# A hybrid decoder layer on one core: small matmuls on column tiles, the forget gate on ScalarE, corrections as biases, and the residuals' mean on GpSimd

## The chip, the cores and the metric

The kernel runs on one core of one Trainium2 chip. The metric is the device time of one execution in microseconds (us); the median of several runs is compared. TensorE (PE in the profile) multiplies matrices, VectorE (DVE), ScalarE (ACT) and GpSimd (POOL) compute elementwise, SyncE (SP) starts transfers.

## The reference

One layer of a decoder (width 2048) is computed for 16 meta tokens, a prompt of 256 tokens and 8 sample tokens, each of which has a past state of its own:

```
x <- LN1(alpha*x + 0.5*SwiGLU_1(x))
x <- LN2(alpha*x + Mixer(x))
x <- LN3(alpha*x + 0.5*SwiGLU_2(x))
Mixer: z = x @ w_in, ten parts of width 2048
  retention (8 heads of 256): rotary q, k; scores q k^T times a decay per head; layer norm per head
  HGRN2 (16 heads of 128): f = lb + (1-lb)*sigmoid(f_h), k = 1 - f, q = silu(q_h), decay prod(f); rms norm per head
  y = sigmoid(a_r)*o_r*silu(g_r) + sigmoid(a_h)*o_h*silu(g_h);  y @ w_out
```

The outputs are the layer's result for the prompt and the samples and the two branches' new states. All inputs are float32, and the feed-forward width is 5504.

## The kernel before, in words

**Dense products.** All 280 tokens lie as columns of tiles with 128 features on the partitions (264 columns where the meta tokens are no longer needed). A weight arrives in units of eight 128x128 blocks (tile `raw`, 512 KB, a transfer of SP's queue, three buffers). ScalarE rounds it to `whi` (L187, type fp32r), VectorE subtracts to get the rest, `wlo` (L188). Activations are split in the same way (`xh`/`xl`, `hh`/`hl`, `yh`/`yl`). Each block then takes three matmuls in `dense` (L217): whi on the high part, whi on the low part, wlo on the high part. A split activation is kept as `Halves`: its left and right half of the columns are read alternately, one column of each in turn, and `pairs` and `apart` lay the output in PSUM out accordingly.

**Order.** The program runs through the first feed-forward layer (`up`, `dn`), norm 1, the mixer, `w_out` (`wo`), norm 2, the second feed-forward layer and norm 3. The order of TensorE's instructions is the order in which the code issues them; the other engines' queues are ordered by a scheduler with priorities. The mixer goes through eight units u, each with one retention head and two HGRN2 heads. A unit's projections are f, q_h, i_h (`pj_f` and so on), then q_r, k_r, v_r, then the gates g_r, a_r, g_h, a_h. `mix_hg` (L717) and `mix_ret` (L952) are generators: after each dense step `pump` counts them down, and a `yield n` asks for n dense steps before the next piece. So the small matmuls stand one group at a time between dense ones, and a group that waits holds all dense work behind it.

**Norm 1 and norm 2.** The first two groups of projections behind a norm multiply x·g before its mean and variance are known. `Norm.first` (L366) and `second` (L383) run them, and `corrected` (L388) puts them right afterwards, with y = -(r·(mean·wg - o)) + wb, where two extra columns of the product give wg and wb. Three VectorE steps do this for each output: a scalar_tensor_tensor, `mul` by r, and at L399 the times -1 plus wb. `first` then goes over the 16 residual tiles d0 to d15: it subtracts the mean at L378 (the helper `sub`, L243) and multiplies by g and r = 1/std at L379. `normalise` (L402) makes the split inputs of everything that follows from these tiles. The mean is the row tile `lnc`, r is `rr`.

**HGRN2.** `evacuate` (L624) turns projections into f, k = 1 - f (both 128x2x280), q and v. f is a sigmoid on ScalarE and a multiply-add on VectorE (L628), k a multiply-add on VectorE (L631). `mix_hg` copies k to K (L723, VectorE), which is later scaled in place. The parts of v are transposed on TensorE for both heads h: two blocks of 128 columns and the 16 columns at each end, four transposes per head into the bank `pt` (L755). The causal scores are built by levels of block size s = 1, 2, 4, 8, 16, 32, 64. The products of neighbours for s = 1 and 2 are split into two tiles and summed over partitions by a matmul with ones (`sums`, L234, banks `pd` and `pl`). For s = 16, 32 and 64 the matmuls K x Q run for each head and block (L803, L798, L793). L803 takes all 128 columns of K at once, so that most of the result is unwanted and a masked VectorE copy (L856, with mask 4) picks the diagonal blocks; L798 puts the two blocks of 32 on two column tiles of the array (`tile_position`), and ScalarE copies the results into `acc` (L851).

**Retention.** After transposes of v and k, `mix_ret` computes the scores `psc` (L996): two wide blocks of 256 and 144 columns and a third with 16 keys and 16 columns. `psr` (L1013) is the new state, seven matmuls of 256 columns per half. Later `pqr` (L1044) multiplies the eight samples' queries, alone in tiles of 32 columns, with their states; samples 0 to 3 and 4 to 7 go to the two halves of a bank, which VectorE adds.

Of the kernel before, what the change touches and what calls it, by code (L numbers as in the profile page):

```python
# [18 lines left out]
P = 128  # L19
# [26 lines left out]
MASKED = 5  # L46

MASKS = {1: [0], 2: [1, MASKED], 4: [2], 8: [3, MASKED + 1], 16: [4]}
# [79 lines left out]
def trunk(ctx: ExitStack, tc: tile.TileContext, A, O):  # L128
# [98 lines left out]
    def sums(out, hilo, part=slice(None)):  # L227

        for i, x in enumerate(hilo):
            if isinstance(x, Halves):  # L230
                o, x = pairs(out), x[:]
            else:
                o, x = out, x[:, part]
            nc.tensor.matmul(o, ones_r, x, start=i == 0, stop=i == 1)  # L234

    def mul(out, a, b):
        nc.vector.tensor_tensor(out=out, in0=a, in1=b, op=ALU.mult)

# [29 lines left out]
    class Norm:  # L268
# [96 lines left out]
        def first(self, block, outs, x0s):  # L365
# [10 lines left out]
            for c in range(KC):  # L376
                d = self.d[c]
                sub(d, d, self.mean)  # L378
# [9 lines left out]
        def corrected(self, outs, x0s, into=()):  # L388
            ys = []
            for i, (o, x0) in enumerate(zip(outs, x0s)):  # L390
# [6 lines left out]
                mul(y, y, self.r[:, x0:])  # L397
                to = into[i] if i < len(into) else y
                nc.vector.tensor_scalar(out=to, in0=y, scalar1=-1.0, scalar2=wgb[:, 1:2], op0=ALU.mult, op1=ALU.add)  # L399
                ys.append(to)  # L400
# [52 lines left out]
    def ffn(i, block, w_dn, which, before=None):  # L453
# [3 lines left out]
        with tc.tile_pool(name=f"h{i}", bufs=1) as hp:  # L457
            hh, hl = [None] * FC, [None] * FC
            for gn, grp in enumerate(ffn_up_groups()):
# [4 lines left out]
                else:  # L464
                    dense(block, KC, outs, xh, xl, cols, parts_in_turn=gn == 0)
                ng = len(grp) // 2
                for j in range(ng):
                    m = grp[j][1]
                    sg = hp.tile([P, n], F32, tag="sg", name=f"sg{m}", bufs=2)
                    nc.scalar.activation(sg, outs[j][:, :n], AF.Silu)  # L470
                    mul(sg, sg, outs[ng + j][:, :n])
# [60 lines left out]
    with tc.tile_pool(name="yp", bufs=1) as yp:  # L532
# [7 lines left out]
        with tc.tile_pool(name="mp", bufs=1) as mp:  # L540
# [37 lines left out]
            vsm = tmp("vsm", (P, 2, P))  # L578
# [26 lines left out]
            def project(groups):  # L605
                for grp in groups:
# [9 lines left out]
                    else:  # L616
                        dense(block, KC, outs, xh, xl, [slice(x0, T) for x0 in x0s], pump)
                    for j in range(0, len(grp), 2):
                        w = T - x0s[j]
                        evacuate(grp[j][0], grp[j][1], grp[j + 1][1], outs[j][:, :w], outs[j + 1][:, :w])  # L620

            def evacuate(n, c0, c1, o0, o1):
                if n == "f":
                    f = tmp("f", (P, 2, T))  # L624
                    k = tmp("k", (P, 2, T))
                    for j, (c, o) in enumerate(((c0, o0), (c1, o1))):
                        nc.scalar.activation(f[:, j, :], o, AF.Sigmoid)
                        nc.vector.tensor_scalar(  # L628
                            out=f[:, j, :], in0=f[:, j, :], scalar1=olb[:, c : c + 1], scalar2=lb[:, c : c + 1],
                            op0=ALU.mult, op1=ALU.add)  # L630
                    nc.vector.tensor_scalar(out=k, in0=f, scalar1=-1.0, scalar2=1.0, op0=ALU.mult, op1=ALU.add)  # L631
# [577 lines left out]
```

## Time and profile before

| what | value |
|---|---|
| median of 3 runs | 2615.33 us (2613.51 to 2615.54) |
| the profiled execution | 2614.54 us, span 2612.5 us, granted TensorE clock 0.999 |
| busy: PE, DVE, ACT, POOL | 2593.6, 1738.4, 1355.4, 3.3 us |
| transfers | 536.26 MB, mean 205 GB/s |
| casts whi and subtractions wlo, all forms | 870 of 1042 ns on ACT, 869 of 1223 ns on DVE |

The profile is one execution. The span goes from its first to its last instruction; some 2 us of the execution lie outside it. A row of a group gives line, engine, operation, output<-inputs and shapes, and then the busy time, the mean of one in ns, and the engine's idle time just before these instructions with what ended it. A row of the waits gives the waiting engine's tile and line, the engine and tile that it waited for, and then the sum in us, the count and the longest. A row of the timeline gives the start, the time up to the last end, and how many instructions of the kind followed one another.

### The profile page before, as it was taken

The page shows a single profiled execution, that of the slowest core. Times are in us where ns is not written, and L with a number is a line of the kernel's source. Part 1 is how long each engine was busy: PE and PEld are TensorE (multiplying, and loading weights), DVE is VectorE, ACT ScalarE, POOL GpSimd, SP SyncE. Part 2 cuts the span into 40 slices and gives each one's busy share as a digit, 9 for nine tenths or more (in the row PEclk, how much of TensorE's full clock was granted, in tenths as well). Part 3 has the DMA queues.
Part 4 walks back from the last instruction along what each step waited for, and adds up shares of the span by engine and source line. Part 5 has one row for each costly group of instructions (what it writes and reads, how often), then busy time and mean ns, then how long its engine had stood idle before and what let it go on. Part 6 is the DMA issues. An engine that isn't in the chain of part 4 may idle for free.

```text
span 2612.5 us, 54486 instructions
## 1 busy us (share of the span) xinstructions
PE 2593.6 (99%) x22576; PEld 2564.1 (98%) x22576; DVE 1738.4 (67%) x2961; ACT 1355.4 (52%) x2120; POOL 3.3 (0%) x38
## 2 busy tenths in 40 slices
PE   9999999999999999999999999999999999999999
PEld 9999999999999999999999999999999999999998
DVE  6554444565579788787878787876995555556555
ACT  5444444444455566656565656565564444444444
POOL 0000000000000000000000000000000000000000
PEclk9999999999999999999999999999999999999999
DMA  7556555556566686767676767666656666666664
GB/s 243 185 185 186 184 184 184 185 186 184 182 195 212 231 271 206 245 212 245 214 249 213 249 215 237 216 232 193 192 181 204 195 197 195 195 194 194 197 198 148
DMA packets 154584, 536.26 MB, mean 205 GB/s; under 512 B 17696, under 2 KB 25696, under 8 KB 154336
## 3 DMA queue, kind: packets, MB, share of 16 engines
q1 hardware_dynamic: 154048, 532.50, 63.4%
q8 instruction: 176, 2.88, 0.4%
q14 instruction: 72, 0.59, 0.1%
q10 hardware_dynamic: 288, 0.29, 0.0%
HBM read 502.12 MB, written 30.61 MB: 204 GB/s over the span
## 4 chain that ended last, share of the span: by engine, by line
PE 89%; DVE 6%; DMA 3%; ACT 2%; issue 1%; SPq 0%; DVEq 0%; ACTq 0%
PE up L217 34%; PE dn L217 18%; PE wo L217 3%; PE pj_q_r L217 3%; PE pj_g_r L217 3%; PE pj_v_r L217 3%; PE pj_f L217 3%; PE pj_k_r L217 3%; PE pj_i_h L217 3%; PE pj_q_h L217 3%; PE pj_a_r L217 3%; PE pj_g_h L217 2%; PE pj_a_h L217 2%; DVE wlo L188 2%; DMA smr<-in_sr 1%
## 5 line engine op out<-in xcount | busy, mean ns | idle before, releaser
L188 DVE TENSOR_TENSOR wlo<-raw,whi 128x1024 fp32r<-128x1024 f32 (+1 forms) x869 | 1061.4, 1223 | 723.5 <-ACT whi L187 721.2
L187 ACT CAST whi<-raw 128x1024 fp32r<-128x1024 f32 (+1 forms) x870 | 904.7, 1042 | 919.4 <-PE up L217 426.7
L217 PE MATMUL up<-xh,wlo 128*128 128x280 f32 (+1 forms) x2624 | 726.0, 280 | 0.8 <-DVE wlo L188 0.6
L217 PE MATMUL up<-xh,whi 128*128 128x280 f32 (+1 forms) x2624 | 725.7, 280 | 0.0
L217 PE MATMUL up<-xl,whi 128*128 128x280 f32 (+1 forms) x2624 | 725.4, 279 | 0.0
L217 PEld LDWEIGHTS up<-xh,wlo 128*128 128x128 f32 x2624 | 492.6, 189 | 1.7 <-DVE wlo L188 1.6
L217 PEld LDWEIGHTS up<-xh,whi 128*128 128x128 f32 x2624 | 492.8, 189 | 0.0
L217 PEld LDWEIGHTS up<-xl,whi 128*128 128x128 f32 x2624 | 492.6, 189 | 0.0
L217 PE MATMUL dn<-hh,whi 128*128 128x280 f32 (+1 forms) x1376 | 384.7, 280 | 0.0
L217 PE MATMUL dn<-hl,whi 128*128 128x280 f32 (+1 forms) x1376 | 384.3, 279 | 0.0
L217 PE MATMUL dn<-hh,wlo 128*128 128x280 f32 (+1 forms) x1376 | 384.3, 279 | 0.0
L217 PEld LDWEIGHTS dn<-hh,whi 128*128 128x128 f32 x1376 | 260.1, 189 | 0.1
L217 PEld LDWEIGHTS dn<-hl,whi 128*128 128x128 f32 x1376 | 260.1, 189 | 0.1
L217 PEld LDWEIGHTS dn<-hh,wlo 128*128 128x128 f32 x1376 | 260.1, 189 | 0.0
L217 PE MATMUL pj_g_r<-xh,whi 128*128 128x264 f32 x256 | 76.7, 300 | 0.0
L217 PE MATMUL pj_v_r<-xh,whi 128*128 128x280 f32 x256 | 74.3, 290 | 0.0
L217 PE MATMUL pj_g_h<-xh,whi 128*128 128x264 f32 x256 | 73.5, 287 | 0.0
L217 PE MATMUL pj_k_r<-xh,wlo 128*128 128x280 f32 x256 | 72.7, 284 | 0.3
L217 PE MATMUL pj_k_r<-xh,whi 128*128 128x280 f32 x256 | 72.7, 284 | 0.0
L217 PE MATMUL pj_v_r<-xl,whi 128*128 128x280 f32 x256 | 72.7, 284 | 0.0
L217 PE MATMUL pj_v_r<-xh,wlo 128*128 128x280 f32 x256 | 72.7, 284 | 0.0
L217 PE MATMUL pj_g_h<-xh,wlo 128*128 128x264 f32 x256 | 71.0, 277 | 1.6 <-DVE wlo L188 1.6
(401 smaller groups left out, 5281.5 us busy)
## 6 DMA issues: line engine op xcount, KB each, us to landing
raw<-in_w_up SPq DMA_DIRECT2D x343, 512.0 KB, 3.9
raw<-in_w_in SPq DMA_DIRECT2D x320, 512.0 KB, 4.1
raw<-in_w_dn SPq DMA_DIRECT2D x172, 512.0 KB, 3.5
smr<-in_sr SPq DMA_DIRECT2D x32, 512.0 KB, 5.3
out_srs<-smr SPq DMA_DIRECT2D x32, 512.0 KB, 5.1
raw<-in_w_out SPq DMA_DIRECT2D x32, 512.0 KB, 3.5
smh<-in_sg SPq DMA_DIRECT2D x16, 512.0 KB, 4.5
vbr<-vrd SPq DMA_DIRECT2D x16, 512.0 KB, 5.6
```

Of the source, the lines that this page charges most:

```text
L187: nc.scalar.copy(hi[:, j:jn, :], raw[:, j:jn, :])
L188: nc.vector.tensor_tensor(out=lo[:, j0:j1, :], in0=raw[:, j0:j1, :], in1=hi[:, j0:j1, :].bitcast(F32), op=ALU.subtract)
L217: nc.tensor.matmul(o, w, t, start=start, stop=stop)
```

## The change

1. **Norms 1 and 2.** `first` subtracts the mean from d0 to d15 with `nc.gpsimd` in place of VectorE; multiplying by g and r stays on VectorE. In `corrected` the `mul` by r becomes a scalar_tensor_tensor that also multiplies by -1. The last step, adding wb, goes away: `corrected` returns (y, wb), and the consumers take wb as the bias of their ScalarE activation or as a scalar of their VectorE multiplication (`mul_biased`). Only v, in `second`, still has it added at once.
2. **Forget gate.** The multiply-add for f, the one for k, and the copy from k to K go to ScalarE.
3. **Transposes of v.** GpSimd collects the ends of v for both heads in a tile `ends` (128 x 64 elements), which one transpose then turns; per unit there are five transposes in place of eight.
4. **Level 16** runs on four column tiles of the array with 32 columns each, in 16 matmuls of 16 columns; ScalarE copies the results as for s = 32. Mask 4 goes, and with it its part of the transfer and the cast at the start. **Level 64** puts its two blocks b on two column tiles.
5. **Third score.** It moves from `psc` to the bank of `pqr`, right ahead of its matmuls, and its product with the decay and its split move along. The two halves of `pqr` now sum up in the bank, and the VectorE addition goes.
6. **Order of columns.** The moving operands of `sums` with two parts (`pd` and s = 2) and of `psr` are read alternately from their two halves, as in `dense`; the readers of the result take the columns apart again.

The diff, cut to its core:

```diff
-MASKED = 5
-MASKS = {1: [0], 2: [1, MASKED], 4: [2], 8: [3, MASKED + 1], 16: [4]}
+MASKED = 4
+MASKS = {1: [0], 2: [1, MASKED], 4: [2], 8: [3, MASKED + 1]}
 ...
     def sums(out, hilo, part=slice(None)):
+            elif len(x.shape) == 3 and x[:, part].shape[1] == 2:
+                o, x = pairs(out), x[:, part].rearrange("p a b -> p b a")
 ...
+    def mul_biased(out, o, b, x):
+        if b is None:
+            mul(out, x, o)
+        else:
+            nc.vector.scalar_tensor_tensor(out=out, in0=o, scalar=b, in1=x, op0=ALU.add, op1=ALU.mult)
 ...
         def first(self, block, outs, x0s):
-                sub(d, d, self.mean)
+                nc.gpsimd.tensor_tensor(out=d, in0=d, in1=self.mean, op=ALU.subtract)
 ...
         def corrected(self, outs, x0s, into=()):
-                mul(y, y, self.r[:, x0:])
-                to = into[i] if i < len(into) else y
-                nc.vector.tensor_scalar(out=to, in0=y, scalar1=-1.0, scalar2=wgb[:, 1:2], op0=ALU.mult, op1=ALU.add)
-                ys.append(to)
+                nc.vector.scalar_tensor_tensor(out=y, in0=y, scalar=-1.0, in1=self.r[:, x0:], op0=ALU.mult, op1=ALU.mult)
+                if i < len(into):
+                    nc.vector.tensor_scalar(out=into[i], in0=y, scalar1=wgb[:, 1:2], scalar2=None, op0=ALU.add)
+                ys.append((y, wgb[:, 1:2]))
 ...
-                        nc.scalar.activation(f[:, j, :], o, AF.Sigmoid)
-                        nc.vector.tensor_scalar(
-                            out=f[:, j, :], in0=f[:, j, :], scalar1=olb[:, c : c + 1], scalar2=lb[:, c : c + 1],
-                            op0=ALU.mult, op1=ALU.add)
-                    nc.vector.tensor_scalar(out=k, in0=f, scalar1=-1.0, scalar2=1.0, op0=ALU.mult, op1=ALU.add)
+                        nc.scalar.activation(f[:, j, :], o, AF.Sigmoid, **bias(b))
+                        nc.scalar.activation(f[:, j, :], f[:, j, :], AF.Identity, scale=olb[:, c : c + 1], bias=lb[:, c : c + 1])
+                    nc.scalar.activation(k, f, AF.Identity, scale=-1.0, bias=1.0)
 ...
             def mix_hg(u, f, k, q, v):
+                ends = tmp("ends", (P, 2, 2, NMETA))
+                nc.gpsimd.tensor_copy(ends[:, :, 0, :], v[:, :, :NMETA])
+                nc.gpsimd.tensor_copy(ends[:, :, 1, :], v[:, :, T - NMETA :])
-                nc.vector.tensor_copy(K, k[:, :, :LP])
+                nc.scalar.copy(K, k[:, :, :LP])
 ...
-                    for b, (t0, n) in enumerate(((NMETA, P), (NMETA + P, P), (0, NMETA), (T - NMETA, NMETA))):
-                        nc.tensor.transpose(pt[:n, b * P : (b + 1) * P], v[:, h, t0 : t0 + n], ident)
+                    for b in range(2):
+                        nc.tensor.transpose(pt[:, b * P : (b + 1) * P], v[:, h, NMETA + b * P : NMETA + (b + 1) * P], ident)
+                    x = pt[:64, 2 * P : 3 * P]
+                    if h:
+                        nc.tensor.transpose(x, ends.rearrange("p c a t -> p (c a t)"), ident)
 ...
                             if s == 64:
+                                j = 64 * b
                                 nc.tensor.matmul(
-                                    pl[0:s, o : o + s], K[:, h, k0 : k0 + s], Q[:, h, q0 + s : q0 + 2 * s],
-                                    start=True, stop=True)
-                            elif s == 32:
-                                for j in (0, 64):
+                                    pl[j : j + s, h * s : (h + 1) * s], K[:, h, k0 : k0 + s], Q[:, h, q0 + s : q0 + 2 * s],
+                                    start=True, stop=True, tile_position=(0, j))
+                            else:
+                                for j in range(0, P, 2 * s):
                                     nc.tensor.matmul(
                                         pl[j : j + s, o : o + s], K[:, h, k0 + j : k0 + j + s],
                                         Q[:, h, q0 + j + s : q0 + j + 2 * s], start=True, stop=True, tile_position=(0, j))
 ...
-                        nc.tensor.matmul(pst[:, :256], kk, vv, start=i == 0, stop=i == 6)
+                        nc.tensor.matmul(pairs(pst[:, :256]), kk, vv.rearrange("p c f -> p f c"), start=i == 0, stop=i == 6)
 ...
                 pq = mx_bank("pqr")
+                scores(pq[:, 256:], 2)
-                                pq[32 * j : 32 * j + 32, 256 * e : 256 * e + 256], qdr[:, c, 32 * b : 32 * b + 32],
-                                sms[2 * e + c][:, j, :], start=c == 0, stop=c == 1, tile_position=(0, 32 * j))
+                                pq[32 * j : 32 * j + 32, :256], qdr[:, c, 32 * b : 32 * b + 32],
+                                sms[2 * e + c][:, j, :], start=e + c == 0, stop=e + c == 2, tile_position=(0, 32 * j))
+                mul(scr2[:NB2], pq[:NB2, 256 : 256 + NMETA], dt[:NB2, c2:])
+                upper_upper_lower(sc2, scr2[:NB2])
-                add(os, os, pq[:, 256:])
```

The order of VectorE's queue right behind the statistics of norm 1, before the change. `lnc` holds the mean, `rt` and `rr` lead to 1/std, the d tiles are residuals, and `p` is the bank with the sum of squares:

```order
L237 TENSOR_TENSOR lnq<-lnc 128x280
L243 TENSOR_TENSOR d_5931<-d_5931,lnc 128x280
L362 SCALAR_TENSOR_TENSOR lnq<-p_8743,lnq 128x280
L243 TENSOR_TENSOR d_6110<-d_6110,lnc 128x280
L243 TENSOR_TENSOR d_6126<-d_6126,lnc 128x280
L243 TENSOR_TENSOR d_6307<-d_6307,lnc 128x280
L243 TENSOR_TENSOR d_6482<-d_6482,lnc 128x280
L243 TENSOR_TENSOR d_6657<-d_6657,lnc 128x280
L188 TENSOR_TENSOR wlo_8861<-raw_8859,whi_8860 128x8x128
```

The same place in the changed kernel, up to the first multiplications by g and r (L390):

```order
L239 TENSOR_TENSOR lnq<-lnc 128x280
L373 SCALAR_TENSOR_TENSOR lnq<-p_8743,lnq 128x280
L188 TENSOR_TENSOR wlo_8861<-raw_8859,whi_8860 128x8x128
L239 TENSOR_TENSOR rt<-rr 128x280
L264 SCALAR_TENSOR_TENSOR rt<-rt,rv 128x280
L265 SCALAR_TENSOR_TENSOR rr<-rt,rr 128x280
L188 TENSOR_TENSOR wlo_8891<-raw_8889,whi_8890 128x8x128
L390 SCALAR_TENSOR_TENSOR d_5931<-d_5931,lnp,rr 128x280
L390 SCALAR_TENSOR_TENSOR d_6110<-d_6110,lnp,rr 128x280
```

The subtractions have left VectorE's queue, `wlo` of the next weights and the steps to 1/std have moved up, and the multiplications of d still stand ahead of the `wlo` that follow them. On GpSimd the subtractions now stand in one row, behind an instruction without operands that the build puts there (ISA):

```order
L591 MEMSET qdr 128x512
L389 ISA
L389 TENSOR_TENSOR d_5931<-d_5931,lnc 128x280
L389 TENSOR_TENSOR d_6110<-d_6110,lnc 128x280
L389 TENSOR_TENSOR d_6126<-d_6126,lnc 128x280
```

On TensorE, in the fifth unit, before: level 16 (bank `pl`) and the scores of retention (`psc`), each between dense matmuls:

```order
L217 MATMUL pj_v_r_16143<-xh_9_9268,wlo_16225 128x280
L803 MATMUL pl<-Q,K 128x64 x4
...
L217 MATMUL pj_a_r_16301<-xh_8_9264,wlo_16436 128x264
L996 MATMUL psc<-q_r,k_r 128x256 x2
L996 MATMUL psc<-q_r,k_r 128x144 x2
L996 MATMUL psc<-q_r,k_r 16x16 x2
L217 MATMUL pj_g_r_16300<-xh_9_9268,whi_16435 128x264
```

After, the same two places, and further on the start of `pqr`:

```order
L217 MATMUL pj_v_r_16197<-xh_9_9264,wlo_16279 128x280
L825 MATMUL pl<-Q,K 16x16 x16
...
L217 MATMUL pj_a_r_16370<-xh_8_9260,wlo_16505 128x264
L1024 MATMUL psc<-q_r,k_r 128x256 x2
L1024 MATMUL psc<-q_r,k_r 128x144 x2
L217 MATMUL pj_g_r_16369<-xh_9_9264,whi_16504 128x264
...
L217 MATMUL pj_a_r_16844<-xh_10_9268,wlo_16925 128x264
L1024 MATMUL pqr<-q_r,k_r 16x16 x2
L1073 MATMUL pqr<-smr,qdr 32x256 x16
L217 MATMUL pj_g_r_16843<-xh_11_9272,whi_16924 128x264
```

The two instructions of the third score have moved from the end of `psc` to right ahead of `pqr`; level 16 (L825) has 16 instructions of 16 columns where L803 had four of 64, at the same place between dense matmuls, and the number of `pqr` matmuls is the same.

More of the change, by code (lines that the diff above doesn't have):

```diff
@@ L848, in mix_hg @@
                         pass
-                    elif s >= 32:
+                    elif s == 64:
+                        for b in range(2):
+                            nc.scalar.copy(
+                                acc[:s, :].rearrange("p (h b n s) -> p h b n s", h=2, b=2, s=s)[:, :, b, 1, :],
+                                pl[b * s : (b + 1) * s, : 2 * s].rearrange("p (h s) -> p h s", h=2))
+                    elif s >= 16:
                         for j in range(0, 128 // s, 2):
@@ L993, in mix_ret, with scores @@
                 psc = mx_bank("psc")
[L994 removed]
+                def scores(out, b):
+                    _, l0, n, nk = SCORES[b]
                     for c in range(2):
                         nc.tensor.matmul(
[L997 to L998 removed]
+                            out[:nk, :n], k[:, c, b * P : b * P + nk], q[:, c, l0 : l0 + n], start=c == 0, stop=c == 1)
+                for b in range(2):
+                    scores(psc[:, SCORES[b][0] :], b)
                 scr = dt
```

74 lines of the change are left out of this document (38 added, 36 removed).

## The prediction

> **What bounds the kernel now.** I read the page first, then the waits of TensorE, then the chain that ended last, then windows of the stretches where TensorE waits, and last the timeline around the small matmuls.
>
> ```profile
> PE 2593.6 (99%) x22576; PEld 2564.1 (98%) x22576; DVE 1738.4 (67%) x2961; ACT 1355.4 (52%) x2120; POOL 3.3 (0%) x38
> 1834.71 62.52 PE wo L217 x555
> 517.40 228.09 PE dn L217 x1914
> PE pl L793 <- DVE Q L237: 2.3, 1, 2.3
> PE pj_g_h L217 <- DVE wlo L188: 1.6, 3, 0.7
> PE psr L1013 <- DVE ks L985: 1.3, 2, 0.7
> PE pl L803 <- DVE K L237: 1.2, 1, 1.2
> PE pt L979 <- DVE acch L779: 1.2, 1, 1.2
> PE pd L234 <- DVE prodvbh L225: 0.9, 1, 0.9
> PE pd L234 <- ACT prodsmh L224: 0.8, 1, 0.8
> ```
>
> The first row says that TensorE (PE) is busy 99% of the span. A matmul's busy time overlaps its neighbour's here, so what counts is the distance between starts. The next two rows, stretches of the chain, give it: 62.52 us for 555 matmuls of 264 columns is **113 ns** each, 228.09 us for 1914 of 280 columns is **119 ns**. A column costs 0.426 ns either way. So the end moves by what leaves TensorE's stream and by what TensorE no longer waits. The waits by releaser, in us, count and longest, add up to 9.3 us in these seven rows; the matmul before a wait also does not overlap with the next one, so the real loss is a little larger. Nearly all of it is VectorE (DVE) being late; the one row that names ScalarE is a cast that itself had waited for a VectorE product.
>
> ```profile
> 787.00:818.00 31.00, 29.11 (x235) 27.81 (x234) 30.94 (x67) 15.01 (x30) 0.00 (x0) 1.00 0.57 179
> 1240.00:1371.00 131.00, 131.00 (x1171) 128.24 (x1170) 102.65 (x211) 80.69 (x152) 0.00 (x0) 1.00 0.70 231
> 1905.00:1957.00 52.00, 51.67 (x451) 51.08 (x450) 50.57 (x102) 32.78 (x56) 0.00 (x0) 1.00 0.56 177
> ```
>
> These window rows give the length and then the busy us of PE, PEld, DVE, ACT and POOL. VectorE is full in exactly two places: from norm 1 to the first mixer unit (30.94 of 31) and in norm 2 (50.57 of 52). In a settled unit (second row) it has 28 us to spare and ScalarE 50. A profiled execution took 2614.54 us for a span of 2612.5; the median of the runs shown is 2615.33. I sum against 2614.54, 0.8 below that median, well inside the 0.2% (5.2 us) that a measurement of this kernel can tell from no change.
>
> **The change, part by part.** First TensorE's stream, in the fifth of the eight units, between dense neighbours:
>
> ```profile
> 1275.75 0.28 PE L217 MATMUL pj_q_r<-xh,wlo 128*128 128x264 f32 x1
> 1275.86 0.60 PE L755 MATMUL pt<-ident,v 128*128 128x128 f32 x4
> 1276.41 0.28 PE L217 MATMUL pj_q_r<-xl,whi 128*128 128x264 f32 x1
> 1306.46 0.28 PE L217 MATMUL pj_v_r<-xh,wlo 128*128 128x280 f32 x1
> 1306.58 1.00 PE L803 MATMUL pl<-Q,K 128*128 128x64 f32 x8
> 1307.59 0.28 PE L217 MATMUL pj_v_r<-xl,whi 128*128 128x280 f32 x1
> 1313.00 0.28 PE L217 MATMUL pj_a_r<-xh,wlo 128*128 128x264 f32 x1
> 1313.21 0.45 PE L798 MATMUL pl<-Q,K 128*32 128x32 f32 x16
> 1313.80 0.28 PE L217 MATMUL pj_g_r<-xl,whi 128*128 128x264 f32 x1
> 1319.62 0.28 PE L217 MATMUL pj_a_r<-xh,wlo 128*128 128x264 f32 x1
> 1319.73 1.71 PE L996 MATMUL psc<-q_r,k_r 128*128 128x256 f32 x12
> 1321.59 0.28 PE L217 MATMUL pj_g_r<-xl,whi 128*128 128x264 f32 x1
> 1322.04 0.28 PE L217 MATMUL pj_a_r<-xh,wlo 128*128 128x264 f32 x1
> 1322.24 0.68 PE L793 MATMUL pl<-Q,K 128*64 128x64 f32 x8
> 1323.07 0.28 PE L217 MATMUL pj_g_r<-xl,whi 128*128 128x264 f32 x1
> ```
>
> From the dense matmul ahead of a group to the second one behind it there are two dense distances; what is left is the group with the emptying and refilling of the array around it.
>
> - *Transposes of v.* 1276.41 - 1275.75 = 0.66, less 2 x 0.113, is 0.43 us for four, 0.109 each, whether 128 or 16 columns are held. Eight per unit become five: **-0.33 us**. It cannot be less unless the 64-column one costs more than a full one.
> - *Level 16.* 1.13 - 2 x 0.119 = 0.89 us now. Afterwards it is four tiles of 32 columns with 16 moving columns, 32 passes. Level 32 shows the form with two tiles: 0.80 - 0.226 = 0.57 us for 16 passes, 0.45 of it from first start to last end. Two tiles take a pair of passes every 32 ns or so (16 passes in about 0.26 plus 0.3 for changing the array's division and back). Four tiles should take a quadruple in some 45 ns: 8 x 0.045 + 0.3 = 0.66, **-0.23**. Ends: with tiles no better than pairs 16 x 0.032 + 0.3 = 0.81 (-0.08), and no dearer than level 32 (-0.32).
> - *Level 64.* 1.03 - 0.226 = 0.80 us for eight passes one behind the other. Two tiles side by side halve the 0.5 that is not change-over: 0.57 to 0.6, **-0.2**; ends 0 and -0.25.
> - *The third score.* psc takes 1.97 - 0.226 = 1.74 us. Its wide matmuls have 4 x 256 + 4 x 144 = 1600 columns at two clocks, 1600 x 0.852 ns = 1.36. The 16-column score thus costs 0.38, nearly all change-over. Ahead of pqr, whose 32-column tiles pay that change-over anyway, four passes at 25 ns remain: **-0.28**, ends 0 and -0.35.
>
> ```profile
> 1284.05 0.28 PE L217 MATMUL pj_q_r<-xh,wlo 128*128 128x264 f32 x1
> 1284.16 0.40 PE L234 MATMUL pd<-prodsmh,ones_r 128*128 128x512 f32 x1
> 1284.40 0.40 PE L234 MATMUL pd<-prodvbh,ones_r 128*128 128x512 f32 x1
> 1284.63 0.28 PE L234 MATMUL pl<-prodsmh,ones_r 128*128 128x256 f32 x1
> 1323.63 0.99 PE L1013 MATMUL psr<-vs,ks 128*128 128x256 f32 x7
> 1324.46 0.28 PE L217 MATMUL pj_g_r<-xh,whi 128*128 128x264 f32 x1
> ```
>
> - *Interleaved columns.* The dense matmuls read their moving operand alternately from two halves and pay 0.426 ns a column. pd, which reads straight through, takes 0.235 for 512 columns (0.459), psr 0.83 / 7 = 0.119 for 256 (0.463). At 0.426 they take 0.218 and 0.109: four of the first and fourteen of the second per unit, **-0.07 and -0.14**. The new halves lie 256 and 128 elements apart, a distance that no matmul of this trace has; so from -0.21 to a loss of as much again as they take now, 0.94 + 1.66 us per unit.
>
> Sum per unit 0.33 + 0.23 + 0.2 + 0.28 + 0.21 = 1.25, times eight: **-10 us**, with 6 to 11 for all but the interleaving's far end. The number of pqr matmuls stays, so adding both halves in the bank is worth nothing to TensorE.
>
> Now VectorE and what takes its work:
>
> ```profile
> L243 DVE TENSOR_TENSOR d<-d,lnc 128x280 f32<-128x280 f32 x18 | 7.4, 443 | 0.0
> L628 DVE TENSOR_SCALAR f<-f,olb,lb 128x280 f32<-128x280 f32 x16 | 6.6, 420 | 0.0
> L723 DVE COPY K<-k 128x544 f32<-128x544 f32 x8 | 3.5, 441 | 0.2 <-PE ptk L872 0.2
> L399 DVE TENSOR_SCALAR lnq<-lnq,wgb 128x264 f32<-128x264 f32 x4 | 1.4, 352 | 0.0
> L187 ACT CAST whi<-raw 128x1024 fp32r<-128x1024 f32 x867 | 903.3, 1044 | 919.4 <-PE up L217 426.7 <-PE dn L217 224.3 <-issue 55.5
> L577 POOL MEMSET qdr<- 128x512 f32 x1 | 0.5, 529 | 0.0
> ```
>
> - *Off VectorE in norm 1 and the first unit:* 16 subtractions at 7.4 / 18 = 0.41, 6.6 us; six correction steps at 0.35, 2.1; two steps for f at 0.41, k and K at about 0.44 each, 1.7. That is 10.4 us where VectorE has no idle time. In norm 2: 16 x 0.40 + 8 x 0.35 = 9.2 us.
> - *Off VectorE in each settled unit:* the same 1.7, one masked copy and one addition, under 3 of 102 us, beside idle time. Worth nothing except at the pj_g_h waits.
> - *Onto ScalarE:* k and K at the cast's 1.02 ns an element, 0.57 and 0.55, two steps for f at some 0.5, and four copies for level 16: 3 to 4 us per unit, hidden in its 50 us of idle time. Without that cover the whi casts, and behind them wlo, would come up to 4 us late in a unit.
> - *Onto GpSimd (POOL):* the trace has no two-input operation there. The memset writes 512 elements in 0.529, 1.03 ns each; 280 elements are 0.29 as one stream (the lower end) and 0.87 as three streams in turn (the upper). I take two streams, 0.58, since two reads share what the write can overlap. Sixteen are ready 9 us after the mean. VectorE's scaling of d0 to d15, with the wlo of the next weights queued behind each, then meets finished tiles: it needs 1/std first, 7 us after the mean. The two small copies of v's ends precede their transpose by 1.1 us of dense work; a late one costs TensorE that difference, a few tenths per unit.
> - *Start of the program:* the mask's transfer and cast shrink by a fifth. No wait of TensorE above names them; worth nothing.
>
> If VectorE gains the full 10.4 us, the pd and psr waits (3.0) go. The level 64 wait also hangs on a transfer, the others in part on VectorE work of the next unit. I count half of the 9.3, rounded up to **-5 us**; ends 0 and, with the lost overlap, -11.
>
> A rule speaks against the subtraction. The Trainium skill, page "SBUF — State Buffer", section "Who interferes with whom", says that a VectorE instruction with two SBUF inputs and a GpSimd instruction that reads SBUF block each other for the whole instruction. No row here shows both at once. By it the stall part would be given back, as in the first rival. The page "GPSIMD Engine Reference", section 3.1, gives about 2.6 cycles per element at 1.2 GHz for two inputs; my estimate from it is 0.61 us for 280 elements, and the sum would be the same.
>
> **The rivals.**
> 1. *VectorE and GpSimd take turns.* Most VectorE work in the two full stretches reads two SBUF tiles. If each subtraction holds VectorE for its 0.58, that is 9.3 us per norm against 10.4 and 9.2 gained: the waits stay as they are, 2614.5 - 10 = **2604.5**. For it: VectorE has no gaps there to fit them in. Against: nothing in the trace.
> 2. *GpSimd sets the pace, ending slower.* The scaling of d waits in VectorE's queue and every wlo behind it waits too; with weights only three buffers ahead, TensorE follows. From 1.08 us of held VectorE per subtraction (32 x 1.08 - 19.6 = 15, which beats the 10 and the 5.2) the kernel is slower; at 1.3 it is 32 x 1.3 - 19.6 = 22 late, **2626.5**. Against: it is above my upper end of 0.87.
> 3. *The change does not shorten the stream.* The interleaved reads at 128 and 256 elements are slower, or the tiles gain nothing: half the stream part lost, and late parts elsewhere, about **2611**.
>
> **How the numbers follow.** Forecast 2614.5 - 10 - 5 = **2599.5**, chance 0.60. Rival 1 0.22, rival 2 0.06, rival 3 0.10, something between 0.02. The range goes down to all waits gone, 2614.5 - 11 - 11 = 2592, and up past rival 1 to subtractions of 0.75 us (4.4 more): 2609. Faster: forecast, rival 1 and a little of rival 3, 0.85; same: most of rival 3, 0.09; slower: 0.06.
>
> **What would show it.** TensorE's groups between dense neighbours: transposes at 0.109 each, level 16 near 0.66, level 64 near 0.6, pd at 0.218, psr at 0.109; no 16-column score behind psc. VectorE below 95% from 787 to 818 and in norm 2, no pd or psr waits. Rival 1 would show as wlo or scaling steps well above their usual length while POOL runs; rival 2 as VectorE idle with d as releaser. I am wrong if the level 16 and 64 groups stay near 0.8, or if new waits of TensorE name ends, K or f.

## The result, and the profile after

The changed kernel took **2620.86 us** (median of 12 runs, 2616.51 to 2624.91) against 2615.25 before (12 runs, 2611.17 to 2618.09): a ratio of **1.0022** (95% interval 1.0014 to 1.0030). It is slower by 5.6 us; 2599.5 was forecast, and the range ended at 2609. Its profiled execution took 2623.13 us with a span of 2621.3.

I read the page first. This row stands where 2593.6 us of PE and 3.3 us of POOL stood before:

```profile
PE 2590.2 (99%) x22744; PEld 2559.4 (98%) x22744; DVE 1724.7 (66%) x2875; ACT 1380.7 (53%) x2184; POOL 46.3 (2%) x86
```

It tells little: TensorE is full again, with 168 more instructions. The waits of TensorE tell more (us in total, count, longest):

```profile
PE pj_g_h L217 <- DVE wlo L188: 5.8, 9, 0.8
PE pj_i_h L217 <- DVE wlo L188: 3.4, 1, 3.4
PE up L217 <- DVE wlo L188: 3.2, 1, 3.2
PE psr L1041 <- DVE ks L1012: 1.9, 3, 1.0
PE pvr L236 <- ACT rhi L224: 1.8, 2, 1.2
PE pvr L236 <- DVE rlo L225: 1.7, 2, 0.9
```

Three rows are new or much longer, and all three name `wlo`: one wait of 3.4 us behind norm 1 (pj_i_h), one of 3.2 us behind norm 2 (up), and nine short ones at pj_g_h, which came to 1.6 us before. The pd waits of before (1.7 us) are gone, as forecast; those of psr, which were to go too, are not (1.9 us, before 1.3). All waits of TensorE together come to 25.0 us, before to 12.2.

**The stretch behind norm 1.** First GpSimd's row for the 32 subtractions, from the groups by line, then VectorE's timeline in the same stretch (start, us, instructions, idle time before):

```profile
L389 POOL TENSOR_TENSOR d<-d,lnc 128x280 f32<-128x280 f32 (+1 forms) x32 | 34.2, 1105 | 103.5 <-ACT lnc L370 103.5
```

```profile
756.20 1.03 DVE L239 TENSOR_TENSOR lnq<-lnc 128x280 f32<-128x280 f32 x1
757.27 0.45 DVE L373 SCALAR_TENSOR_TENSOR lnq<-p,lnq 128x280 f32<-128x280 f32 x1
759.31 1.87 DVE L188 TENSOR_TENSOR wlo<-raw,whi 128x1024 fp32r<-128x1024 f32 x1 [1.59 <-PE pj_q_h L217]
761.11 1.03 DVE L239 TENSOR_TENSOR rt<-rr 128x280 f32<-128x280 f32 x1
762.17 0.92 DVE L264 SCALAR_TENSOR_TENSOR rt<-rt,rv 128x280 f32<-128x280 f32 x1
763.96 1.80 DVE L188 TENSOR_TENSOR wlo<-raw,whi 128x1024 fp32r<-128x1024 f32 x1
765.68 4.80 DVE L390 SCALAR_TENSOR_TENSOR d<-d,lnp,rr 128x280 f32<-128x280 f32 x5
770.41 1.79 DVE L188 TENSOR_TENSOR wlo<-raw,whi 128x1024 fp32r<-128x1024 f32 x1
772.12 2.71 DVE L390 SCALAR_TENSOR_TENSOR d<-d,lnp,rr 128x280 f32<-128x280 f32 x5
774.75 1.22 DVE L188 TENSOR_TENSOR wlo<-raw,whi 128x1024 fp32r<-128x1024 f32 x1
```

GpSimd works from 755.4 to 772.8, 1.1 us for each tile. In that time `wlo` takes 1.8 us, and 1.22 again at 774.75; a product with both inputs in SBUF takes 1.03 where 0.42 is usual. The row at 757.27 reads `p`, a bank of PSUM, as one of its inputs, and keeps its 0.45. So what is slowed is VectorE's work with two inputs in SBUF. That is the rule of the Trainium skill, page "SBUF — State Buffer", section "Who interferes with whom", which the prediction weighed; the trace agrees with it as to which instructions are slowed. That each instruction holds up the other for its whole length does not quite come out: 16 subtractions at the 0.75 us that one takes alone (measured below) and VectorE's two-input rows of the stretch at their usual lengths, some 8 us, make 20 us, and the stretch took 17.4.

TensorE and its clock in the same stretch and in norm 2, by windows (length; busy us of PE, PEld, DVE, ACT, POOL; granted clock; DMA):

```profile
768.00:772.00 4.00, 0.88 (x8) 0.67 (x6) 4.00 (x4) 1.43 (x4) 4.00 (x5) 0.87 0.16 64
772.00:778.00 6.00, 5.75 (x26) 5.75 (x27) 6.00 (x12) 0.76 (x1) 0.84 (x1) 0.52 0.41 127
778.00:787.00 9.00, 9.00 (x80) 9.00 (x79) 9.00 (x19) 8.99 (x17) 0.00 (x0) 1.00 0.55 179
1924.00:1928.00 4.00, 0.82 (x8) 0.62 (x7) 4.00 (x5) 1.10 (x2) 4.00 (x4) 1.00 0.07 23
1928.00:1932.00 4.00, 4.00 (x23) 4.00 (x22) 4.00 (x9) 0.00 (x0) 0.09 (x1) 0.57 0.40 131
```

TensorE stands for more than 3 us in both norms and then runs at half clock: 26 matmuls in the 6 us from 772, where full speed gives 51, and 23 in the 4 us from 1928, where it gives 36. That adds some 3 and 1.5 us to the waits.

**The small matmuls**, in the fifth unit again, each group from the dense matmul ahead of it to the second one behind; the last two rows are `pqr` in the kernel before:

```profile
1311.40 0.28 PE L217 MATMUL pj_v_r<-xh,wlo 128*128 128x280 f32 x1
1311.61 0.39 PE L825 MATMUL pl<-Q,K 128*16 128x16 f32 x32
...
1312.15 0.28 PE L217 MATMUL pj_v_r<-xl,whi 128*128 128x280 f32 x1
...
1324.17 0.28 PE L217 MATMUL pj_a_r<-xh,wlo 128*128 128x264 f32 x1
1324.29 1.52 PE L1024 MATMUL psc<-q_r,k_r 128*128 128x256 f32 x8
...
1325.75 0.28 PE L217 MATMUL pj_g_r<-xl,whi 128*128 128x264 f32 x1
...
1326.20 0.28 PE L217 MATMUL pj_a_r<-xh,wlo 128*128 128x264 f32 x1
1326.41 0.45 PE L820 MATMUL pl<-Q,K 128*64 128x64 f32 x8
...
1327.01 0.28 PE L217 MATMUL pj_g_r<-xl,whi 128*128 128x264 f32 x1
...
1352.40 0.28 PE L217 MATMUL pj_a_r<-xh,wlo 128*128 128x264 f32 x1
1352.60 0.24 PE L1024 MATMUL pqr<-q_r,k_r 128*16 128x16 f32 x3
...
1354.76 0.28 PE L217 MATMUL pj_g_r<-xl,whi 128*128 128x264 f32 x1
```

```profile
1348.56 0.28 PE L217 MATMUL pj_a_r<-xh,wlo 128*128 128x264 f32 x1
...
1351.08 0.28 PE L217 MATMUL pj_g_r<-xl,whi 128*128 128x264 f32 x1
```

Less the two dense distances, level 16 takes 0.75 - 0.24 = 0.51 us (0.89 before), `psc` 1.58 - 0.23 = 1.35 (1.74), level 64 0.81 - 0.23 = 0.58 (0.80), and `pqr` 2.36 - 0.23 = 2.13 although the third score now stands in it (2.52 - 0.23 = 2.29). The transposes of v take 0.55 together (0.87). `pd` stands at 0.22 a matmul, and from the first `psr` to the dense matmul behind it are 0.78 us (0.83). A unit's stream is shorter by 0.38 + 0.39 + 0.22 + 0.16 + 0.32 + some 0.15 = 1.6 us, **13 us** for eight. The stream did what was forecast, and more; waits and half clock ate it.

**The settled units.** ScalarE's row that ends a long idle time there, in the changed kernel:

```profile
1363.97 1.06 ACT L1058 ACTIVATE smr<-smr 128x1024 f32<-128x1024 f32 x1 [5.03 <-DMA smr<-in_sr]
```

This scaling of the next unit's states (tile `smr`) waits for their load; `whi` of the next weights stands behind it in ScalarE's queue, and `wlo` and pj_g_h behind that. The load was issued at 1357.44, so it took 6.5 us. Before, it was issued at 1354.16 and the scaling began at 1358.76, 4.6 us later. For the first load of each of the fourth to eighth units, the time from issue to scaling is 6.5 to 7.4 us (mean 6.9); before it is 4.6 to 5.6 (mean 5.1).

### The profile page after: what moved, and what is told of

Same layout as the page of the kernel before. It is cut to its first block, busy times and chain, and to the rows that moved or that the text cites. A ratio compares the mean times of both kernels' runs of the same rounds, so it can differ in the third digit from the quotient of the medians.

```text
span 2621.3 us, 54862 instructions
## 1 busy us (share of the span) xinstructions
PE 2590.2 (99%) x22744; PEld 2559.4 (98%) x22744; DVE 1724.7 (66%) x2875; ACT 1380.7 (53%) x2184; POOL 46.3 (2%) x86
## 4 chain that ended last, share of the span: by engine, by line
PE 90%; DVE 4%; DMA 3%; ACT 2%; issue 1%; SPq 0%; DVEq 0%; ACTq 0%
PE up L217 36%; PE dn L217 18%; PE pj_v_r L217 4%; PE wo L217 3%; PE pj_k_r L217 3%; PE pj_g_r L217 3%; PE pj_i_h L217 3%; PE pj_q_h L217 3%; PE pj_a_r L217 3%; PE pj_f L217 3%; PE pj_q_r L217 3%; PE pj_g_h L217 2%; PE pj_a_h L217 2%; DMA smr<-in_sr 2%; DVE wlo L188 2%
## 5 line engine op out<-in xcount | busy, mean ns | idle before, releaser
L217 PE MATMUL pj_k_r<-xl,whi 128*128 128x280 f32 x256 | 72.3, 283 | 0.0
```

The source lines that it names most:

```text
L217: nc.tensor.matmul(o, w, t, start=start, stop=stop)
```

## The experiments

Each ratio is to the kernel before on the same chip, and 0.1% is 2.6 us.

| run | what differs from the changed kernel | median us | ratio (95%) |
|---|---|---|---|
| a_dve_sub | VectorE subtracts | 2610.88 | 0.9984 (0.9975 to 0.9993) |
| a_pad_mask | five masks in memory | 2612.39 | 0.9990 (0.9982 to 0.9999) |
| a_third_back | third score in psc | 2623.20 | 1.0026 (1.0017 to 1.0036) |
| a_dve_pad | VectorE subtracts, five masks | **2605.80** | **0.9957** (0.9944 to 0.9969) |
| a_dve_pad_again | the same, other chip | 2607.15 | 0.9962 (0.9948 to 0.9976) |
| a_gp_half | half of the tiles, five masks | 2609.04 | 0.9978 (0.9969 to 0.9987) |
| a_fkk_pad | a_dve_pad, f, k, K on VectorE | 2606.92 | 0.9967 (0.9955 to 0.9980) |
| b_gp_sub | the kernel *before*, GpSimd subtracts | 2622.86 | 1.0030 (1.0020 to 1.0041) |
| b_small | the kernel *before*, table of four | 2618.58 | 1.0009 (1.0000 to 1.0018) |

**Who subtracts.** Two runs undo and isolate that part. In the changed kernel:

```diff
-                nc.gpsimd.tensor_tensor(out=d, in0=d, in1=self.mean, op=ALU.subtract)
+                sub(d, d, self.mean)
```

> The changed kernel with the 16 subtractions of each norm back on VectorE. Theory A (VectorE and GpSimd slow each other down): in the changed kernel VectorE's scaling of d took 0.95 us instead of 0.42 and wlo 1.8 instead of 1.2 while GpSimd subtracted (17.4 us), and TensorE stood 4.3 us in norm 1 and 3.3 in norm 2 and then ran some 5 and 3 us at half clock. All of that goes here, VectorE gets 13 us of subtractions back, and some of the waits of the first unit return: 2609 to 2613, no wlo longer than 1.3 us, no pj_i_h wait of 3.4. Rival B (the stalls come from the other moves, such as the order of VectorE's queue after the statistics): the waits of 3.4 and 3.2 stay and the time is within 1.5 of 2621.

Measured 2610.88: theory A. The waits of 3.4 and 3.2 us are gone. In the kernel before, the opposite edit and nothing else:

> The kernel before with nothing changed but the 16 subtractions of each norm, which go to GpSimd. Theory A (VectorE and GpSimd slow each other down): the same slow stretch of 17 us in both norms and the same stalls, some 6.9 us with the half clock in norm 1 and 5 in norm 2, of which the first unit gives back 3 to 5 because VectorE has 6.6 us less to do later: 2620 to 2626, slower than before. Rival B (the stalls come from the other moves): 2610 to 2616, since VectorE is relieved where it is full.

Measured 2622.86: theory A again. Its waits show the two stalls of the changed kernel:

```profile
PE up L217 <- DVE wlo L188: 4.6, 3, 3.2
PE pj_i_h L217 <- DVE wlo L188: 3.4, 1, 3.4
```

**Half of the tiles.**

```diff
+                if c < KC // 2:
+                    sub(d, d, self.mean)
+                else:
+                    nc.gpsimd.tensor_tensor(out=d, in0=d, in1=self.mean, op=ALU.subtract)
```

> The changed kernel with five masks in memory and only the tiles d8 to d15 subtracted on GpSimd, d0 to d7 on VectorE. With all 16 on GpSimd it took 2612.4, with none 2605.8. Theory A1 (the price is the time that GpSimd holds VectorE, 0.55 us for each subtraction, all of it in the first 17 us behind the mean, where the wlo of the next weights are due): the slow stretch shrinks to about 9 us, VectorE loses 4.4 there, the waits of 3.4 and 3.2 shrink to 0.5 to 1.5 and the half clock behind them goes: 2606 to 2609. Rival A2 (any GpSimd work there lets the d products or the library load hold the queue): the waits stay above 2.5 and the time is 2611 to 2613.

Measured 2609.04, between the two ends (2605.8 with none on GpSimd, 2612.4 with all, both with five masks) and at the upper edge of theory A1. The longest waits are here:

```profile
PE pj_f L217 <- DVE wlo L188: 2.9, 2, 2.7
PE up L217 <- DVE wlo L188: 2.2, 4, 1.5
```

The one of norm 1 is longer than theory A1 expected (0.5 to 1.5) and would have fitted A2. My reading is that the other eight subtractions now stand in VectorE's queue in the same stretch and are slowed too (five of them take 4.47 us). From 768 to 772, right behind the wait of 2.7 us, the clock stayed at 1.00.

**The price by itself.** Extra GpSimd work on scratch tiles in the second feed-forward layer:

```diff
+                    for _ in range(16):
+                        if gn == 6:
+                            nc.gpsimd.tensor_tensor(out=pa, in0=pa, in1=pb, op=ALU.subtract)
+                        elif gn == 9:
+                            nc.gpsimd.tensor_copy(pa, pb)
+                        else:
+                            nc.gpsimd.memset(pa, 0.0)
```

> The kernel with VectorE's subtractions and five masks in memory, and in the second feed-forward layer, where VectorE is half idle, three rows of extra GpSimd work on scratch tiles of 264 columns (beside the computation, which is whole): 16 subtractions with two inputs in SBUF, 16 copies with one, 16 memsets. Theory A (VectorE's instructions with two inputs in SBUF and GpSimd's take turns): beside the subtractions wlo takes 1.7 to 1.9 us in place of 1.22 and the products with a bank of PSUM as one input stay at 0.43 to 0.5; a subtraction takes 0.5 to 0.6 alone and about 1.1 where VectorE is full. If each GpSimd instruction that reads SBUF does the same, the copies lengthen wlo too; the memsets should not, unless it is the instruction and not its reading that counts.

The rows by tile (minimum/median/maximum in ns, first and last start): the three kinds, each with `wlo` in its stretch.

```profile
L495 POOL TENSOR_TENSOR pa<-pa,pb x16: 752/1212/1795, 2043.9 to 2063.4; 128x264 f32<-128x264 f32 x16
L188 DVE TENSOR_TENSOR wlo<-raw,whi x8: 1224/1224/1271, 2044.5 to 2063.4; 128x1024 fp32r<-128x1024 f32 x8
L497 POOL COPY pa<-pb x16: 409/411/1431, 2108.1 to 2119.0; 128x264 f32<-128x264 f32 x16
L188 DVE TENSOR_TENSOR wlo<-raw,whi x4: 1225/1340/1450, 2109.3 to 2117.4; 128x1024 fp32r<-128x1024 f32 x4
L499 POOL MEMSET pa<- x16: 313/318/319, 2172.8 to 2178.4; 128x264 f32 x16
L188 DVE TENSOR_TENSOR wlo<-raw,whi x4: 1225/1226/1226, 2171.4 to 2179.5; 128x1024 fp32r<-128x1024 f32 x4
```

A subtraction alone takes 0.75 us, and up to 1.8 where `wlo` holds it up; a copy takes 0.41, and `wlo` beside it up to 1.45; memsets slow nothing. Theory A holds, but not as I expected it here: `wlo` beside the subtractions stays at 1.22 to 1.27, and it is GpSimd that waits. Two pairs from the timeline, one of each kind, show who waits:

```profile
2060.66 1.22 DVE L188 TENSOR_TENSOR wlo<-raw,whi 128x1024 fp32r<-128x1024 f32 x1 [1.48 <-ACT whi L187]
2060.70 1.79 POOL L495 TENSOR_TENSOR pa<-pa,pb 128x264 f32<-128x264 f32 x1
2111.97 0.41 POOL L497 COPY pa<-pb 128x264 f32<-128x264 f32 x1
2112.00 1.45 DVE L188 TENSOR_TENSOR wlo<-raw,whi 128x1024 fp32r<-128x1024 f32 x1 [1.31 <-ACT whi L187]
```

The instruction that starts second is the one that takes longer. Where VectorE has no gaps, as behind the means, both engines pay in turn.

**The late loads.** Whether the third score's steps cause the pj_g_h waits:

```diff
-                for b in range(2):
+                for b in range(3):
                     scores(psc[:, SCORES[b][0] :], b)
...
-                scores(pq[:, 256:], 2)
```

> The changed kernel with the third score, its product with the decay and its split back behind the wide scores. In the settled units of the changed kernel the pj_g_h waits on wlo rose from 1.6 to 5.8 us and ate what the shorter stream saved. Theory C (the third score's product and split now stand ahead of whi and wlo on ScalarE and VectorE just where the next weights are due): the pj_g_h waits fall to about 2, the stream grows by 8 x 0.35 = 2.8, so the time stays within 1.5 of 2620. Rival D (the wait hangs on the load of smr, which takes 6.5 us there instead of 4.6, whatever stands in these queues): the pj_g_h waits stay at 5 or more less what the longer stream covers, and the time is 2620 to 2624.

Measured 2623.20, pj_g_h waits 6.5: not theory C but rival D. The next edit leaves every instruction of the mixer alone; the table of masks in memory keeps its fifth mask, and four are loaded:

```diff
-        nc.sync.dma_start(mf[:, :MASKED, :], A["msk"])
+        nc.sync.dma_start(mf[:, :MASKED, :], A["msk"][:, :MASKED, :])
...
-    msk = np.zeros((P, MASKED, 4, 64), np.float32)
+    msk = np.zeros((P, MASKED + 1, 4, 64), np.float32)
```

> The changed kernel with the mask table in memory at its old size of five masks, of which four are loaded. It tests whether the slower loads of smr in the settled units come from where the tensors lie in memory: the table is 131072 bytes smaller in the changed kernel, so that what lies behind it has moved. Theory E (place in memory): smr lands 4.6 us after its issue again, pj_g_h waits fall below 3, time 2616 to 2618. Rival D' (not the place): waits and time as in the changed kernel, within 1.5 of 2621.

Measured 2612.39, better than theory E expected, with pj_g_h waits of 2.1 us; the five loads that took 6.9 us on average in the changed kernel take 5.5. Both edits together:

> The changed kernel with both: the subtractions back on VectorE and the mask table in memory at its old size of five masks. The one alone took 2610.9, the other 2612.4, against 2620.9. Theory E (where the tensors lie in memory sets how fast the loads of the mixer land): it still saves a part of the 8.4 here, since the run with VectorE's subtractions alone had 3.9 us of pj_g_h waits and smr landing 6.4 to 8.3 us after pq: 2603 to 2607. Rival D' (the 8.4 was something else that the subtractions on GpSimd needed): 2609.5 to 2612.

Measured 2605.80, and 2607.15 on another chip: **0.4% faster than the kernel before**, and the best of all. ScalarE's row there, which answers to the one above, and TensorE's longest waits:

```profile
1349.09 1.06 ACT L1058 ACTIVATE smr<-smr 128x1024 f32<-128x1024 f32 x1 [3.10 <-DMA smr<-in_sr]
```

```profile
PE psr L1041 <- DVE ks L1012: 3.7, 3, 2.5
PE pvr L236 <- ACT rhi L224: 2.2, 2, 1.2
PE pvr L236 <- DVE rlo L225: 1.7, 2, 0.9
```

The load was issued at 1344.49 and took 4.6 us, and no pj_g_h wait is left (1.1 us in the run on the other chip). The other direction, in the kernel before, the fifth mask in a tensor behind all others:

> The kernel before with its mask table in memory cut to four masks, the fifth in a tensor of its own behind all others; everything that lies behind the table has the place of the changed kernel, and no instruction changes but one more small load at the start. Theory E (place in memory): smr is scaled 7 to 8 us after pq starts in place of 5.7 to 7.0, the pj_g_h waits rise from 1.6 to 4 or more, 2618 to 2623. Rival D' (not the place): 2614 to 2617, pj_g_h waits below 2.5.

Measured 2618.58: at the lower end of theory E, with pj_g_h waits of 4.4 us and the smr scaling 7.3 to 8.4 us after `pq` in four units of five.

Two more of a_dve_pad, one with a sixth mask in memory, one with f, k and K on VectorE:

> As the one with VectorE's subtractions and a table of five masks in memory, but with six masks (another 131072 bytes behind it moved). It tells whether only the place with four masks is bad or each place has its own time. Theory E, only four is bad: within 1.5 of the run with five masks. Theory E, each place has its own time: 2606 to 2612. Rival D': 2609.5 to 2612 like the run with VectorE's subtractions alone.

> The changed kernel with VectorE's subtractions and five masks in memory (2605.8), and f, k and K back on VectorE. It gives the worth of that part. Theory F (worth only where VectorE is full, in the first unit, 1.7 us of VectorE): 2606 to 2608.5, with longer waits of psr and pl in the first two units. Rival G (ScalarE is now the later engine, since whi is due there): 2603 to 2605.

Measured 2606.54 (0.9963), so of the three sizes tried only the table of four costs time, though this run's pj_g_h waits are 3.3 us, close to the 3.9 of a_dve_sub; and 2606.92, so that f, k and K on ScalarE have no worth that these runs can tell.

**What is it about the table?** Seven kernels with four masks, all with VectorE's subtractions, tried that. An unused tensor of the missing size behind the table, ahead of the states, and ahead of the weights:

```diff
-        "msk": msk.reshape(P, MASKED, 2 * P), "ident": np.eye(P, dtype=np.float32),
+        "msk": msk.reshape(P, MASKED, 2 * P), "gap": np.zeros((P, 2 * P), np.float32), "ident": np.eye(P, dtype=np.float32),
```

> The changed kernel with VectorE's subtractions, four masks in memory, and an unused tensor of 131072 bytes declared right behind the table, so that, if an unused tensor takes its place in memory, all that lies behind has the place of the run with five masks (2605.8) while no instruction differs from the one with VectorE's subtractions alone (2610.9). Theory E3 (place in memory, of what lies between the table and the weights): 2604 to 2607.5, smr scaled 5 to 6.5 us after pq starts. Rival E4 (an unused tensor takes no place, or it is the table's own size that counts): 2609 to 2613.5.

> As the run with the unused tensor behind the table, but with it declared right ahead of the mixer's states, behind the tokens and the small tables. Theory E5 (the place of the states and what follows decides): 2604 to 2607.5. Theory E6 (the place of tokens and constants, or nothing of the kind): 2609 to 2613.5.

> The changed kernel with VectorE's subtractions, four masks in memory, and an unused tensor of 131072 bytes declared behind the inputs of the mixer's states and ahead of all weights. If tensors lie in the order of their declaration, the weights then have the place of the run with five masks (2605.8) and the states, the tokens and the constants that of the changed kernel (2610.9). Theory E1 (the place of the weights decides): 2604 to 2607.5. Theory E2 (the place of the states and the small tables decides, or an unused tensor takes no place): 2609 to 2612.5.

Measured 2610.83 (0.9984), 2610.69 (0.9987) and 2613.39 (0.9993): no effect. A used tensor behind the table, and the load in two halves:

```diff
+        nc.sync.dma_start(mf[:, MASKED, :], A["gap"])
```

```diff
-        nc.sync.dma_start(mf[:, :MASKED, :], A["msk"])
+        nc.sync.dma_start(mf[:, :2, :], A["msk"][:, :2, :])
+        nc.sync.dma_start(mf[:, 2:MASKED, :], A["msk"][:, 2:, :])
```

> The changed kernel with VectorE's subtractions, a table of four masks, and behind it a tensor of 131072 bytes that a load at the start reads (into a part of the mask tile that is overwritten). Theory E3 (place in memory, and the unused tensor took no place): 2604 to 2607.5 like the run with five masks (2605.8), pj_g_h waits below 2. Rival E7 (the table's rows or its load count, not the place): 2609 to 2613.

> The changed kernel with VectorE's subtractions and the table of four masks loaded in two halves, so that no load reads it as one whole piece. No tensor lies elsewhere. Theory E3 (place): 2609 to 2613 like the run with one load (2610.9). Rival E7 (how the table is loaded at the start shifts the order in which later loads are served): 2604 to 2607.5.

Measured 2613.00 (0.9983), against E3, and 2610.84 (0.9971, 0.9961 to 0.9981), against E7, if less clearly. Then two tables of two masks (`"msk"` and `"msl"`, each with its load), and the states moved by 131072 bytes inside their own tensor:

> The changed kernel with VectorE's subtractions and the four masks in two tensors of two masks, each read by a load of its own. The tensors together have the size of the one table of four masks, but no tensor of 524288 bytes is left among the small ones. Theory E8 (it is that tensor's own size, not where the others lie): 2604 to 2607.5, pj_g_h waits below 2.5. Rival E9 (the bytes of all tables together, so place after all): 2609 to 2613, pj_g_h waits of 3.5 or more.

```diff
+    A["sr"] = np.concatenate([np.zeros((P, 256), np.float32), sr])
```

> The changed kernel with VectorE's subtractions and four masks, and retention's sample states moved by 131072 bytes within their own tensor (zeros ahead of them), so that the source of the smr loads lies elsewhere whatever places the tensors get. Theory E10 (the place of the states against the weights decides how fast smr lands): 2604 to 2607.5, smr scaled 5 to 7 us after pq starts, pj_g_h waits below 2.5. Rival E11 (not that place): 2609 to 2613, pj_g_h waits of 3.5 or more.

Measured 2610.64 (0.9981): E9; and 2609.65 (0.9977): E11. All seven stay at 2609.6 to 2613.4 where five or six masks take 2605.8 to 2607.2. **This stays open**: how fast the states land in the mixer, a millisecond later, goes with the size of the table in memory. The mean of the five loads named above is 5.1 to 5.5 us in the eight runs with five masks, 6.0 in the one with six, and 6.1 to 7.0 in the eleven with four. But neither its load, nor the sum of the sizes, nor the place of the states was shown to be the reason, and since the run with six masks lies between in its loads and is fast, the loads alone may not be all that the table changes.

## Why the prediction was wrong

- *TensorE's stream: right, and too small.* Forecast 10 us with 6 to 11 as bounds, measured 13. Level 16 gave 0.38 per unit, not 0.23 (four tiles pack better than I took from two), and the third score gave 0.39 + 0.16, not 0.28. Transposes (0.32) and level 64 (0.22) came as forecast, the interleaved columns at some 0.15 of 0.21. Rival 3 is out.
- *The step that failed: the subtractions as work that runs beside VectorE at no cost to it ("sixteen are ready 9 us after the mean", and VectorE "then meets finished tiles").* They took 17.4 us. The 0.58 us for one was below the 0.75 that the probe shows alone, and the turns with VectorE made it 1.1. Late tiles were not the harm, though: no idle time of VectorE in the changed kernel names GpSimd's `d` as what ended it, so rival 2's path is not what happened. VectorE's own instructions grew longer, and `wlo` came late.
- *Rival 1 had the mechanism, and its price was nearly right; its conclusion was not.* In the timeline of that stretch VectorE loses 0.6 on `lnq`, 0.6 on each of three `wlo`, 2.6 on five products of d (five take 2.2 where GpSimd is idle), and another 2 on the steps to 1/std and the later products: 7 of the 9.3 us that I worked out. But the rival set this against the 10.4 us of work taken away and left TensorE's waits as they were. The work taken away lies over 60 us, the loss within 17 us right where `wlo` is due and three weight buffers are all the cover there is. So one wait of over 3 us came in each norm, and the half clock behind it. Putting the subtractions back on VectorE gained 0.38% with four masks and about 0.3% with five, that is 7 to 10 us.
- *"VectorE's relief, -5 us": not gained.* In a_dve_pad VectorE has, by the prediction's own prices, 3.8 us less to do in norm 1 and the first unit, and yet it is busy 30.89 of the 31 us from 787 to 818, where the forecast had it below 95%. TensorE's waits come to 13.0 us in all (before 12.2), with 3.7 us at psr (before 1.3) and 3.9 at pvr (before 0.7) in place of others. The shorter stream brings TensorE earlier to the same VectorE work; that reading fits, but no run isolates it.
- *Not thought of: the table.* I had called the start of the program worth nothing. Cutting the table from five masks to four costs 5 to 8 us in the changed kernel (a_dve_pad against a_dve_sub, a_pad_mask against the changed kernel), and about 2 in the kernel before, with an interval that reaches down to nothing.

The sum: 2615.3 - 13 for the stream is 2602. The profiled execution of a_dve_pad took 2602.52, its median is 3 us above, which no view of that one execution explains. From 2605.8, the table adds 5 (2610.9, a_dve_sub) and GpSimd's subtractions 10 (2620.9). Against the forecast of 2599.5 that is 3 us gained by the stream, 5 not gained by VectorE's relief, 10 lost to the subtractions and 5 to 8 to the table; 1 to 4 us of the 21 are not accounted for.

## What to carry to other kernels

Before work is moved from VectorE to GpSimd, ask whether both read SBUF in the same stretch, with two inputs on VectorE's side: here the time was then not simply taken off: most of it was handed back in turns, and it came due at once. Compare gain and loss in the window of the wait that ends last, not over the stage. And when waits change in a place whose instructions did not, look at the loads there, and vary the layout of the data in memory once before blaming the code.

## What the hardware showed that I had not expected

- The granted clock fell to one half for 3 to 6 us behind a wait of 3.2 or 3.4 us, and stayed at 1.00 behind one of 2.7 us in the run with half of the tiles. The Trainium skill, page "TensorE: Matmul & The Clock Gate", Part 1, gives an idle window of about 3.4 us for this, and these three waits agree with it roughly. As a threshold for one wait it does not hold here. In the kernel before, the two pd waits of 0.8 and 0.9 us, with one matmul between them, had the same effect (first two rows), and in a_dve_pad so had a single wait of 2.5 us, that of psr which ended at 831.0 (last row):

```profile
812.00:818.00 6.00, 4.39 (x34) 3.87 (x32) 5.94 (x16) 2.91 (x5) 0.00 (x0) 1.00 0.50 160
818.00:822.00 4.00, 3.86 (x17) 3.82 (x18) 4.00 (x10) 0.77 (x3) 0.00 (x0) 0.58 0.50 139
832.00:836.00 4.00, 4.00 (x25) 4.00 (x24) 3.94 (x12) 3.60 (x11) 0.00 (x0) 0.64 0.73 255
```

- A subtraction of two 128x264 tiles costs GpSimd 0.75 us, a copy 0.41, a memset 0.32. Beside memsets no `wlo` took more than 1.23 us; beside copies one took 1.45, and beside the subtractions of norm 1 one took 1.87.
- 128 KB less in a table that is read once at the start made loads of another tensor, a millisecond later, slower: 6.9 us on average in place of 5.5 (the changed kernel against a_pad_mask), and 6.4 in place of 5.1 (a_dve_sub against a_dve_pad). Why is open.
